# The end of a mixture-of-experts layer: residual rows read once and normed between the last expert products, and the last two experts' rows normed apart and stored by index

## The chip, the cores and the metric

The kernel runs on one core of one Trainium2 chip. The metric is the device time of one execution in microseconds (us): 1222.65 us, the median of three runs (1221.38 to 1224.46). The profile is of one further execution, which took 1224.64 us; the profiler's span of it is 1222.9 us. All rows below are from that execution, and their times count from the start of its span. Engines are named as the profile names them: PE is TensorE (PEld its weight loads), DVE is VectorE, ACT is ScalarE, POOL is GpSimd, SP is SyncE, which here only issues DMAs. A "q" behind a name is the engine's sequencer.

## The reference, cut to what matters

One layer over 1024 tokens of width 1024: a mixer, a cross-attention, then a mixture of 16 experts in 4 groups (each token goes to one group and to two experts in it), and a final RMSNorm. Only the last part matters here:

```
x   = x + sum over a token's two experts e of  weight * (silu(t @ w_gate[e]) * (t @ w_up[e])) @ w_down[e]
out = x / sqrt(mean(x * x) + 1e-6) * final_norm          # per token, over 1024 columns
```

Here t is the normed x. The two experts of a token lie in one group, so two experts of different groups never share a token.

## The kernel before, in words

**Experts.** Token rows of t lie in DRAM as `h3d`, the rows of x as `acd`; both are 1024 x 1024 float32 (plus spare rows). `ORDER` runs the experts as 0, 4, 8, 12, 1, 5, ... 11, 15, so neighbours are of different groups. Each expert has a first tile of up to 128 token rows and a second of up to 64 more; the second is computed inside `second(e)` (L1207), a branch that is taken only if the expert has more than 128 tokens. Row numbers are in `idi`, combine weights in `wts`; `slot(e, i)` (L1089) gives both columns for tile i. A row number past the end is left out by the DMA.

**One expert.** `fetch` gathers rows of `h3d` by an indirect DMA on POOL; `turned` transposes them on PE; `gate_up` (L1126) does 6 products of 512 columns for each of 8 weight tiles (48 in all), `hidden` the silu and the product, `over` (L1135) transposes the result into `hid`, `down` (L1143) does 6 products for each of 4 weight tiles (24). For the second tile the like are `gate_up2` (32 products), `hidden2`, `over2`, `down2` (16) and `rows2` (L1194). Every product is done as three, on operands split in a high and a low part (`split`, L173: the high part a copy on ACT, the low part a subtraction on DVE, 128 x 1024 each).

**Rows back.** `add_rows` (L1198) adds an expert's rows to `acd` by an indirect DMA on POOL that accumulates in DRAM. The framework orders whatever touches the same DRAM tensor, so an add waits until the one before it has landed. The loop over the first 15 experts is a software pipeline: while expert `ORDER[s]` is computed, the down products and adds of `ORDER[s-1]` are done (L1343 to L1359).

**Weights.** `Weights` (L1260) is a queue written out by hand: 9 raw tiles of 512 KB that SP loads in the order of `X.jobs`, and 28 slots for split pairs. `X.split(n)` splits the next n loaded tiles and so frees raw tiles for further loads; `X.get(key)` splits until the tile asked for is ready. The order of the jobs (L659 to L665) puts the last expert's gate and up tiles behind the down tiles of the one before. In this data the branches of expert 11 (called `p` at the end) are taken, those of 7 and 15 (`LAST`) are not.

**The end.** After the loop come p's down products and both adds (L1369 to L1381), then the last expert's gate, up and hidden (L1387 to L1395), then SP reads all of `acd` as eight row tiles `acc[t]` (L1402), then its down products. The last expert's rows are not added in DRAM: `placed` (L1433) puts them in place by products with a 0/1 matrix `oh`, 4 to 6 per half tile of 512 columns. Modes "A" and "B" alternate over the tiles: in "A" DVE adds the product to `acc` in SBUF and the norm works on `acc`; in "B" PE adds `acc` by one more product and the norm reads PSUM. `summed` (L1452) is a square with a row sum on ACT and two small operations on POOL (add EPS, power -0.5); `scaled` (L1464) multiplies by the root and by `final_norm` (`fn`) on DVE and SP stores the tile. All of this is under `manual_schedule`: each engine executes its own instructions in program order.

Of the kernel before, what the change touches and what calls it, by code (L numbers as in the profile page):

```python
# [8 lines left out]
F32 = mybir.dt.float32  # L9
F32R = mybir.dt.float32r  # L10
# [43 lines left out]
C_N = C_WR + ND * 24  # L54


MODES = "ABABABAB"
START = 12
FILL = 2
LAG = 2  # L60


class Slots:
# [22 lines left out]
def block_kernel(ctx: ExitStack, tc: tile.TileContext, A):  # L86
# [572 lines left out]
    for s, e in enumerate(ORDER):  # L659
        gu = [("gu", e, k) for k in range(ND)]  # L660
        dn = [("dn", ORDER[s - 1], k) for k in range(4)] if s else []
        for name, i, k in dn + gu if s == NE - 1 else gu + dn:
            W.add((name, i, k), A["w_" + name][i, k])
    for k in range(4):
        W.add(("dn", ORDER[-1], k), A["w_dn"][ORDER[-1], k])  # L665
# [541 lines left out]
    def second(e):  # L1207

        return tc.If((flags & (1 << e)) > 0, preferred_fallthrough_block=True)

    hrow = [half.get() for _ in range(2)]
    routed = half.get(BF16, (P, P))
    act.copy(routed, idf)
# [98 lines left out]
    with tc.manual_schedule():  # L1312
        flags = nc.values_load(two[0:1, 0:1], engines=(PE, ACT, DVE), min_val=0, max_val=(1 << NE) - 1)
        X = Weights(W.jobs, W.flying, W.ready, RAW)
        X.load()
        x0 = x0_bufs[0]
        run(turned(x0, xg[0]))
        with second(ORDER[0]):
            turned2()
        for i in range(2):  # L1320
            fetch(ORDER[1], i)
        pool.memset(og[1][LO], 0.0)
        for s, e in enumerate(ORDER[:-1]):
            p = ORDER[s - 1] if s else None
            nx = ORDER[s + 1]
            for k in range(ND):
                gate_up(x0, X.get(("gu", e, k)), k)
                X.split(1)
            hidden()
            ws = [X.get(("gu", e, k)) for k in range(ND)]  # L1330
            with second(e):
                for k in range(ND):
                    gate_up2(ws[k], k)
                hidden2(slot(e, 1)[1])
            for k in range(ND):
                X.drop(("gu", e, k))
            x0 = x0_bufs[(s + 1) % 2]
            ops = turned(x0, xg[0])
            if s + 2 < NE:
                fetch(ORDER[s + 2], 0)  # L1340
            run(ops)
            X.split(2)
            if p is not None:  # L1343
                wd = [X.get(("dn", p, k)) for k in range(4)]
                for k in range(4):
                    down(wd[k], k)
                X.split(1)
                weighted(slot(p, 0)[1])
                add_rows(slot(p, 0)[0], og[0])
            over()  # L1350
            X.split(2)
            if p is not None:
                with second(p):
                    for k in range(4):
                        down2(wd[k], k)
                    rows2(og[1])
                add_rows(slot(p, 1)[0][LO], og[1][LO])
                for k in range(4):
                    X.drop(("dn", p, k))  # L1359
            with second(e):  # L1360
                over2()
            with second(nx):  # L1362
                turned2()
            if s + 2 < NE:
                fetch(ORDER[s + 2], 1)


        p, LAST = ORDER[-2:]
        wd = [X.get(("dn", p, k)) for k in range(4)]  # L1369
        for k in range(4):  # L1370
            down(wd[k], k)
        X.split(1)
        weighted(slot(p, 0)[1])
        add_rows(slot(p, 0)[0], og[0])
        with second(p):
            for k in range(4):
                down2(wd[k], k)
            rows2(og[1])
        add_rows(slot(p, 1)[0][LO], og[1][LO])
        for k in range(4):  # L1380
            X.drop(("dn", p, k))  # L1381
        slots.put(*xg, *x0_bufs[NE % 2])
        fn, row = slots.get(), slots.get()
        oh = slots.get(F32R), slots.get(F32R)
        pool.iota(row, pattern=[[1, T]], base=0, channel_multiplier=0, allow_small_or_imprecise_dtypes=True)
        pool.dma_start(fn, A["final_norm"])
        for k in range(ND):  # L1387
            gate_up(x0, X.get(("gu", LAST, k)), k)
            X.split(2)
# [8 lines left out]
        assert not X.jobs  # L1398
        X.split(4)
        wd = [X.get(("dn", LAST, k)) for k in range(4)]  # L1400
        acc = [X.place(X.raw, F32) for _ in range(NT)]
        for t in range(NT):  # L1402
            sp.dma_start(acc[t], acd[cut(t), :])
        over()
        with second(LAST):
            over2()
        slots.put(*x0, xp)
        slots.free.extend(X.raw)
        ogs = [[slots.get(F32R) for _ in range(2)] for _ in range(2)]
        for i in range(2):  # L1410
            dve.tensor_scalar(oh[i], row, idf[:, LAST * 8 + i:LAST * 8 + i + 1], None, op0=ALU.is_equal)
        with second(LAST):
            for k in range(4):
                down2(wd[k], k)
            rows2(og[1])
            split(ogs[1][0][LO], ogs[1][1][LO], og[1][LO])
        for k in range(4):
            down(wd[k], k)
        for n in range(2):
            split(ogs[0][0][:, HS[n]], ogs[0][1][:, HS[n]], dn_banks[n], slot(LAST, 0)[1])  # L1420
        for k in range(4):
            X.drop(("dn", LAST, k))
        slots.free.extend(X.pair)
        slots.put(*og, hid, hp)
        banks.put(*gu_banks, *dn_banks, *turn_banks)

    ssf = const.tile([P, 2 * NT], F32, name="ssf")
    rf = const.tile([P, NT], F32, name="rf")  # L1430
    pss, jk = {}, {}

    def placed(t):  # L1433
        jk[t] = slots.get()
        pss[t] = [banks.get() for _ in range(2)]
        for n, ps in enumerate(pss[t]):
            pe.matmul(ps, oh[0][:, cut(t)], ogs[0][0][:, HS[n]], start=True, stop=False)
        with second(LAST):
            for n, ps in enumerate(pss[t]):
                for o in ogs[1]:  # L1440
                    pe.matmul(ps, oh[1][LO, cut(t)], o[LO, HS[n]], start=False, stop=False)
        for n, ps in enumerate(pss[t]):
            pe.matmul(ps, oh[0][:, cut(t)], ogs[0][1][:, HS[n]], start=False, stop=MODES[t] != "B")  # L1443
            if MODES[t] == "B":
                pe.matmul(ps, ident, acc[t][:, HS[n]], start=False, stop=True)  # L1445

    def added(t):
        if MODES[t] != "B":
            for n, ps in enumerate(pss[t]):
                dve.tensor_tensor(acc[t][:, HS[n]], ps, acc[t][:, HS[n]], op=ALU.add)  # L1450

    def summed(t):  # L1452
        r, s2 = rf[:, t:t + 1], [ssf[:, 2 * t + n:2 * t + n + 1] for n in range(2)]
        if MODES[t] == "B":
            for n, ps in enumerate(pss[t]):
                act.activation(jk[t][:, HS[n]], ps, AF.Square, scale=1.0 / 32.0, accum_out=s2[n])  # L1456
            pool.tensor_scalar(r, s2[0], s2[1], EPS, op0=ALU.add, op1=ALU.add)  # L1457
        else:
            act.activation(jk[t], acc[t], AF.Square, scale=1.0 / 32.0, accum_out=s2[0])
            pool.tensor_scalar(r, s2[0], EPS, None, op0=ALU.add)  # L1460
        pool.tensor_tensor(r, r, mhalf[:, 0:1], op=ALU.pow)
        slots.put(jk[t])

    def scaled(t):  # L1464
        r = rf[:, t:t + 1]
        if MODES[t] == "A":
            dve.scalar_tensor_tensor(acc[t], acc[t], r, fn, op0=ALU.mult, op1=ALU.mult)
        elif MODES[t] == "B":
            for n, ps in enumerate(pss[t]):
                dve.scalar_tensor_tensor(acc[t][:, HS[n]], ps, r, fn[:, HS[n]], op0=ALU.mult, op1=ALU.mult)  # L1470
        else:
            act.activation(acc[t], acc[t], AF.Copy, scale=r)
            pool.tensor_tensor(acc[t], acc[t], fn, op=ALU.mult)
        banks.put(*pss[t])
        sp.dma_start(A["out"][cut(t), :], acc[t])

    with tc.manual_schedule():
        for t in range(NT + LAG):
            if t < NT:
                placed(t)  # L1480
                added(t)
                summed(t)
            if t >= LAG:
                scaled(t - LAG)


def layout(inputs):
# [63 lines left out]
```

## Time and profile before

| | us |
|---|---|
| median of the runs | 1222.65 |
| the profiled execution | 1224.64 |
| its span | 1222.9 |
| PE busy in the span | 1178.0 (96%) |
| DVE busy | 712.3 (58%) |
| ACT busy | 567.5 (46%) |
| POOL busy | 188.6 (15%) |

How to read it: PE is busy nearly everywhere, but the share is a mean over all stages. The last 66 us, from the end of the loop over the experts on, are what the change touches; the table by stretches and the timelines below show them. A timeline row gives start, duration, engine, line, operation, what it writes and reads, how many instructions were merged, and in brackets the engine's idle time before it with what ended it.

### The profile page before, as it was taken

The page shows a single profiled execution, that of the slowest core. Times are in us where ns is not written, and L with a number is a line of the kernel's source. Part 1 is how long each engine was busy: PE and PEld are TensorE (multiplying, and loading weights), DVE is VectorE, ACT ScalarE, POOL GpSimd, SP SyncE. Part 2 cuts the span into 40 slices and gives each one's busy share as a digit, 9 for nine tenths or more (in the row PEclk, how much of TensorE's full clock was granted, in tenths as well). Part 3 has the DMA queues.
Part 4 walks back from the last instruction along what each step waited for, and adds up shares of the span by engine and source line. Part 5 has one row for each costly group of instructions (what it writes and reads, how often), then busy time and mean ns, then how long its engine had stood idle before and what let it go on. Part 6 is the DMA issues. An engine that isn't in the chain of part 4 may idle for free. (4 is left out here: it accounts for less than half of the span.)

```text
span 1222.9 us, 20592 instructions
## 1 busy us (share of the span) xinstructions
PE 1178.0 (96%) x7918; PEld 966.8 (79%) x7918; DVE 712.3 (58%) x1162; ACT 567.5 (46%) x965; POOL 188.6 (15%) x229
## 2 busy tenths in 40 slices
PE   9999999999999999999999999789999999999985
PEld 7787878787889988898888888568787777787762
DVE  6625454547457512364454776756867768668645
ACT  6613232323335402463244443545866767658633
POOL 1100101010100100100001333212223222123122
PEclk9999999999999999999999999889999999999988
DMA  9601110111426811120032321667979779798764
GB/s 343 240 18 48 41 54 35 36 53 54 157 85 242 281 63 35 35 104 1 1 121 83 125 104 70 218 232 242 317 245 377 254 263 349 255 338 290 247 176 194
DMA packets 58316, 196.48 MB, mean 161 GB/s; under 512 B 8925, under 2 KB 9565, under 8 KB 58208
## 3 DMA queue, kind: packets, MB, share of 16 engines
q1 hardware_dynamic: 45216, 157.69, 35.2%
q0 software_dynamic: 12704, 37.26, 10.4%
q8 instruction: 68, 1.11, 0.4%
q14 instruction: 40, 0.33, 0.1%
q10 hardware_dynamic: 288, 0.09, 0.0%
HBM read 173.49 MB, written 29.62 MB: 166 GB/s over the span
## 5 line engine op out<-in xcount | busy, mean ns | idle before, releaser
L257 PE MATMUL b<-s,s 128*128 128x512 f32 (+1 forms) x1056 | 402.7, 382 | 0.9 <-ACT s L165 0.8
L259 PE MATMUL b<-s,s 128*128 128x512 f32 (+1 forms) x1056 | 392.6, 372 | 0.0
L258 PE MATMUL b<-s,s 128*128 128x512 f32 (+1 forms) x1056 | 392.1, 371 | 0.1
L169 DVE TENSOR_TENSOR s<-s,s 128x1024 fp32r<-128x1024 f32 (+2 forms) x272 | 315.1, 1203 | 57.1 <-ACT s L163 35.4
L163 ACT CAST s<-s 128x1024 fp32r<-128x1024 f32 (+2 forms) x272 | 268.2, 1042 | 133.5 <-PE b L259 47.7
L1124 PE MATMUL b<-s,s 128*128 128x512 f32 x1152 | 275.3, 397 | 4.5 <-PEq L1362 1.7
L1124 PEld LDWEIGHTS b<-s,s 128*128 128x128 f32 x1152 | 217.0, 191 | 51.9 <-ACT s L163 2.7
L259 PEld LDWEIGHTS b<-s,s 128*128 128x128 f32 x1056 | 199.0, 188 | 35.4 <-issue 0.2
L257 PEld LDWEIGHTS b<-s,s 128*128 128x128 f32 x1056 | 199.0, 189 | 33.5 <-ACT s L165 1.5
L258 PEld LDWEIGHTS b<-s,s 128*128 128x128 f32 x1056 | 199.5, 189 | 31.3 <-DVE s L171 1.0
L169 DVE TENSOR_TENSOR s<-b,s 128x512 fp32r<-128x512 f32 (+1 forms) x112 | 70.9, 647 | 45.5 <-ACT s L163 42.5
L1200 POOL DMA_INDIRECT acd<-s,idi x30 | 59.2, 1972 | 204.9 <-ACT s L1148 66.4
L1163 PE MATMUL b<-s,s 128*128 128x512 f32 x384 | 90.5, 391 | 0.0
L1163 PEld LDWEIGHTS b<-s,s 128*128 128x128 f32 x384 | 71.6, 188 | 14.7
L163 ACT CAST s<-b 128x512 fp32r<-128x512 f32 (+1 forms) x112 | 60.7, 558 | 42.6 <-PE b L264 16.6
L1106 POOL DMA_INDIRECT s<-h3d,idi x32 | 37.1, 1160 | 106.4 <-PE b L1114 87.3
L1175 ACT COPY h<-b 64x512 f32<-64x512 f32 x32 | 18.6, 582 | 67.7 <-PE b L1163 57.0
L1176 DVE TENSOR_TENSOR h<-b,h 64x512 f32<-64x512 f32 x16 | 10.9, 682 | 63.1 <-ACT h L1175 63.1
L784 DVE TENSOR_TENSOR s<-b,s 128x512 f32<-128x512 f32 x16 | 11.0, 691 | 58.7 <-PE b L259 58.6
L264 PE MATMUL b<-ident,s 128*128 128x128 f32 x288 | 40.9, 273 | 1.0 <-DVE s L615 0.9
L547 DVE TENSOR_TENSOR s<-s,s 128x512 f32<-128x512 f32 x28 | 19.3, 691 | 37.6 <-PE b L538 22.1
L264 PEld LDWEIGHTS b<-ident,s 128*128 128x128 f32 x288 | 34.5, 140 | 8.0 <-DVE s L615 1.3
(232 smaller groups left out, 920.2 us busy)
## 6 DMA issues: line engine op xcount, KB each, us to landing
s<-in_w_gu_dram SPq DMA_DIRECT2D x128, 512.0 KB, 6.8
s<-in_w_dn_dram SPq DMA_DIRECT2D x64, 512.0 KB, 7.5
s<-in_w_in_dram SPq DMA_DIRECT2D x26, 512.0 KB, 3.5
s<-in_w_kv_dram SPq DMA_DIRECT2D x16, 512.0 KB, 5.5
h3d<-s POOLq DMA_DIRECT2D x9, 512.0 KB, 3.1
acd<-s POOLq DMA_DIRECT2D x9, 512.0 KB, 3.2
s<-in_xT_dram SPq DMA_DIRECT2D x16, 256.0 KB, 5.5
s<-in_x_dram SPq DMA_DIRECT2D x8, 512.0 KB, 9.0
```

The source lines that it names most:

```text
L163: act.copy(hi, src)
L169: (eng or dve).tensor_tensor(lo, src, hi.bitcast(F32), op=ALU.subtract)
L257: pe.matmul(ps, lh, rh, start=first, stop=False)
L258: pe.matmul(ps, lh, rl, start=False, stop=False)
L259: pe.matmul(ps, ll, rh, start=False, stop=last)
L264: pe.transpose(pt[:, cut(c)], src[:, cut(half * 4 + c)], ident)
L547: dve.tensor_tensor(k4[:, :, 0, :], k4[:, :, 0, :], tv[:, :, 1:2].to_broadcast([P, nb, w]), op=ALU.mult)
L1106: pool.indirect_dma_start(out=to, out_offset=None, in_=h3d, in_offset=rows, bounds_check=T - 1, oob_is_err=False)
L1124: pe.matmul(ps[n], l, r[:, HS[n]], start=a, stop=b)
L1163: pe.matmul(ps[n], l, r[:, HS[n]], start=first and i == 0, stop=last and i == 1)
L1175: act.copy(up2[UP], ps[UP])
L1200: pool.indirect_dma_start(out=acd, in_=src, in_offset=None, compute_op=ALU.add, out_offset=rows, bounds_check=T - 1, oob_is_err=False)
```

## The change

The order of the jobs in the weight queue becomes gate and up before down for the last expert too. In the last round of the loop the two splits behind `over` go. After the loop the last expert's gate and up products come first, with one split for each weight tile instead of two; when nothing is left to load and five raw tiles are free, SP is given the eight reads of `acd` (into four slots that the loop no longer needs and four raw tiles), and POOL the load of `final_norm`. Then the end goes as follows. POOL gathers three row tiles out of `acd`: p's first tile and the last expert's first tile (`ax[0]`, `ax[1]`), and one tile `ax2` whose lower half are p's second rows and whose upper half the last expert's second rows (`ix2`). The products with `oh` are gone, as are p's two adds into `acd`. In the code below `residual` has SP read `acd` into `acc`; `root` is POOL's two operations (a sum with EPS and a power); `final` calls `summed` for each tile of its list and `scaled` one tile behind; `first_out` scales one `ax[j]` on DVE and calls `store`; `second_out` scales the two halves of `ax2` on DVE, each in its expert's branch, and calls `store` once. A row that neither p nor LAST touches is final in `acc`; all eight tiles of `acc` are normed and stored, and the rows of p and LAST are then stored once more, over them, by three indirect DMAs on POOL. All tiles are normed in mode "A".

```diff
-MODES = "ABABABAB"
+MODES = "AAAAAAAA"
...
-        for name, i, k in dn + gu if s == NE - 1 else gu + dn:
+        for name, i, k in gu + dn:
...
-            X.split(2)
+            if nx != ORDER[-1]:
+                X.split(2)
...
+        def squares(a, ss):
+            act.activation(jk[0:a.shape[0], 0:a.shape[1]], a, AF.Square, scale=1.0 / 32.0, accum_out=ss)
+
+        def summed(t):
+            squares(acc[t], ssf[:, t:t + 1])
+            root(rf[:, t:t + 1], ssf[:, t:t + 1])
+
+        def scaled(t):
+            r = rf[:, t:t + 1]
+            if MODES[t] == "A":
+                dve.scalar_tensor_tensor(acc[t], acc[t], r, fn, op0=ALU.mult, op1=ALU.mult)
...
+            sp.dma_start(A["out"][cut(t), :], acc[t])
...
+        def first_sum(j, e):
+            a, ss, r = ax[j], [ssf[:, NT + 2 * j + n:NT + 2 * j + n + 1] for n in range(2)], rf[:, NT + j:NT + j + 1]
+            for n in range(2):
+                dve.scalar_tensor_tensor(a[:, HS[n]], dn_banks[n], slot(e, 0)[1], a[:, HS[n]],
+                                         op0=ALU.mult, op1=ALU.add)
+                squares(a[:, HS[n]], ss[n])
+            root(r, *ss)
+
+        def second_sum(j, e, wd):
+            part = UP if j else LO
+            with second(e):
+                for k in range(4):
+                    down2(wd[k], k)
+                for n in range(2):
+                    act.copy(up2[UP], gu1_banks[n][UP])
+                    dve.tensor_tensor(og[1][part, HS[n]], gu1_banks[n][LO], up2[UP], op=ALU.add)
+                dve.tensor_tensor(ax2[part], ax2[part], og[1][part], op=ALU.add)
+                act.activation(jk[part], ax2[part], AF.Square, scale=1.0 / 32.0, accum_out=c1[0][0][part])
+
+        def store(ix, src):
+            rows = bass.IndirectOffsetOnAxis(ap=ix, axis=0)
+            pool.indirect_dma_start(out=A["out"], in_=src, in_offset=None, out_offset=rows,
+                                    bounds_check=T - 1, oob_is_err=False)
...
+            X.split(1)
+            if not X.jobs and len(X.raw) >= 5 and len(acc) == 4:
+                residual(range(4))
+                acc += [X.place(X.raw, F32) for _ in range(4)]
+                residual(range(4, NT))
+                fn = X.place(X.raw, F32)
+                pool.dma_start(fn, A["final_norm"])
...
         X.split(4)
...
+        for ix, to in (slot(p, 0)[0], ax[0]), (slot(LAST, 0)[0], ax[1]), (ix2, ax2):
+            pool.indirect_dma_start(out=to, out_offset=None, in_=acd,
+                                    in_offset=bass.IndirectOffsetOnAxis(ap=ix, axis=0))
+        for k in range(4):
+            down(wd[k], k)
         over()
+        first_sum(0, p)
+        second_sum(0, p, wd)
         with second(LAST):
             over2()
...
+        final(range(0, 4))
+        second_sum(1, LAST, wl)
+        root(c1[1], c1[0][0])
         for k in range(4):
...
+            down(wl[k], k)
+        final(range(4, NT))
+        first_out(0, p)
+        second_out()
+        first_sum(1, LAST)
+        first_out(1, LAST)
```

## Rows read from the trace of the kernel before

**Rows 1.** The table by stretches for three stretches of the last 53 us: length, then busy time (and instructions) of PE, PEld, DVE, ACT and POOL, then PE's granted clock, the DMA share and GB/s.
```profile
1170.00:1180.00 10.00, 8.17 (x34) 5.81 (x32) 8.31 (x9) 8.58 (x10) 3.56 (x3) 1.00 0.36 55
1180.00:1190.00 10.00, 6.41 (x19) 4.91 (x20) 4.92 (x6) 0.88 (x2) 1.75 (x3) 0.66 0.83 222
...
1210.00:1223.00 13.00, 0.99 (x3) 0.16 (x1) 4.19 (x6) 1.57 (x6) 2.47 (x4) 0.74 0.39 161
```
**Rows 2.** The timeline of PE: a gate and up of 48 products, the transposes of `over`, those of `over2`, p's 24 down products and its 16 of the second tile, and the 24 down products of the last expert.
```profile
1107.55 11.16 PE L1124 MATMUL b<-s,s 128*128 128x512 f32 x48 [0.27 <-PEq L1362]
...
1155.26 0.60 PE L1139 MATMUL b<-ident,h 128*128 128x128 f32 x4
1156.27 0.46 PE L1188 MATMUL b<-ident,h 64*128 64x64 f32 x4 [0.41 <-PEq L1353]
1157.14 5.95 PE L1124 MATMUL b<-s,s 128*128 128x512 f32 x24 [0.42 <-ACT s L163]
1162.93 3.79 PE L1163 MATMUL b<-s,s 128*128 128x512 f32 x16
...
1184.71 7.73 PE L1124 MATMUL b<-s,s 128*128 128x512 f32 x24 [0.72 <-ACTq L1405]
```
**Rows 3.** The timeline of the norm of the first tile, of mode "A": the square on ACT and POOL's two operations.
```profile
1196.05 1.06 ACT L1459 ACTIVATE s<-s 128x1024 f32<-128x1024 f32 x1 [2.53 <-DVE s L1450]
...
1197.30 0.24 POOL L1460 TENSOR_SCALAR rf<-ssf 128x1 f32<-128x1 f32 x1 [15.54 <-ACT s L1459]
...
1197.62 0.58 POOL L1461 TENSOR_TENSOR rf<-rf,mhalf 128x1 f32<-128x1 f32 x1
```
**Rows 4.** The timeline of DVE and POOL at the end of the norms: L1467 scales a tile of mode "A" (both inputs in SBUF), L1470 two halves of mode "B" (one input in PSUM).
```profile
1210.18 1.40 DVE L1470 SCALAR_TENSOR_TENSOR s<-b,rf,s 128x512 f32<-128x512 f32 x2
...
1210.40 0.22 POOL L1460 TENSOR_SCALAR rf<-ssf 128x1 f32<-128x1 f32 x1 [1.97 <-ACT s L1459]
...
1211.50 1.28 DVE L1467 SCALAR_TENSOR_TENSOR s<-s,rf,s 128x1024 f32<-128x1024 f32 x1
...
1211.82 1.13 POOL L1457 TENSOR_SCALAR rf<-ssf 128x1 f32<-128x1 f32 x1 [0.55 <-ACT s L1456]
1213.03 0.56 POOL L1461 TENSOR_TENSOR rf<-rf,mhalf 128x1 f32<-128x1 f32 x1
1213.62 1.41 DVE L1470 SCALAR_TENSOR_TENSOR s<-b,rf,s 128x512 f32<-128x512 f32 x2 [0.84 <-POOL rf L1461]
```
**Rows 5.** Instructions of the kernel's closing line (L1547) by engine: count, shortest, median and longest in ns, first and last start; then what SP waited for in the last part: in all, times, longest.
```profile
L1547 POOLq DRAIN  x3: 46/109/9029, 1213.0 to 1222.6; - x3
...
SPq L1547 <- PEq L1547: 4.6, 2, 4.1
...
SPq L1547 <- DMA out_dram<-s: 1.9, 1, 1.9
```
**Rows 6.** The timeline of POOL around the last adds into `acd`.
```profile
1156.89 2.15 POOL L1200 DMA_INDIRECT acd<-s,idi  x1 [15.51 <-ACT s L1148]
1167.85 1.43 POOL L1200 DMA_INDIRECT acd<-s,idi  x1 [8.81 <-DMA acd<-s,idi]
1171.11 1.56 POOL L1200 DMA_INDIRECT acd<-s,idi  x1 [1.82 <-DMA acd<-s,idi]
...
1180.58 1.17 POOL L1386 DMA_DIRECT2D s<-in_final_norm_dram  x1
```
**Rows 7.** From the views by line, the times from issue to landing (shortest, median, longest, in us) with the line's issues: the add at 1167.85 alone, one gather of `h3d` while little else is moved, two gathers back to back under load, the eight reads of `acd`, and the stores of `out`.
```profile
L1200 POOL DMA_INDIRECT acd<-s,idi x1: 1434/1434/1434, 1167.9 to 1167.9; - x1
...
DMA to landing us min/median/max: 2.5/2.5/2.5
...
L1106 POOL DMA_INDIRECT s<-h3d,idi x1: 1039/1039/1039, 1100.8 to 1100.8; - x1
...
DMA to landing us min/median/max: 4.3/4.3/4.3
...
L1106 POOL DMA_INDIRECT s<-h3d,idi x2: 982/1012/1043, 1071.4 to 1072.7; - x2
...
DMA to landing us min/median/max: 6.3/7.0/7.8
...
L1403 SPq DMA_DIRECT2D s<-acd x8: 326/540/872, 1183.5 to 1188.0; - x8
...
DMA to landing us min/median/max: 5.6/8.2/10.1
...
L1475 SPq DMA_DIRECT2D out_dram<-s x8: 332/332/451, 1201.6 to 1215.1; - x8
...
DMA to landing us min/median/max: 2.6/2.7/3.3
```
**Rows 8.** Groups of instructions by line from 1105 to 1182 us (busy time, mean ns of one, idle before): the splits of weights, and the copy and the sum of a second tile.
```profile
L169 DVE TENSOR_TENSOR s<-s,s 128x1024 fp32r<-128x1024 f32 x38 | 44.0, 1216 | 1.4 <-ACT s L163 0.8 <-DVEq L1362 0.6
...
L1175 ACT COPY h<-b 64x512 f32<-64x512 f32 x6 | 3.5, 582 | 10.7 <-PE b L1163 7.2 <-DVE s L1176 3.5
L1176 DVE TENSOR_TENSOR s<-b,h 64x512 f32<-64x512 f32 x4 | 2.7, 683 | 9.3 <-DMA acd<-s,idi 7.9 <-ACTq L1360 0.7 <-ACT h L1175 0.7
```
**Rows 9.** From the view by line, as in rows 7, the earlier plain stores of 512 KB into `acd` from POOL.
```profile
L1029 POOL DMA_DIRECT2D acd<-s x8: 589/589/602, 665.5 to 766.4; - x8
...
DMA to landing us min/median/max: 2.9/3.2/5.5
```

More of the change, by code (lines that the diff above doesn't have):

```diff
@@ L1209, in second @@
         return tc.If((flags & (1 << e)) > 0, preferred_fallthrough_block=True)
+    ssf = const.tile([P, NT + 8], F32, name="ssf")
+    rf = const.tile([P, NT + 4], F32, name="rf")
+    ix2 = const.tile([P, 1], I32, name="ix2")
+    pool.memset(ssf, 1.0)
     hrow = [half.get() for _ in range(2)]
@@ L1368, in block_kernel @@
         p, LAST = ORDER[-2:]
[L1369 to L1381, printed above, removed]
-        slots.put(*xg, *x0_bufs[NE % 2])
@@ L1383, in block_kernel, with residual @@
[L1383 to L1386, printed above, removed]
+        assert p // 4 != LAST // 4
+        slots.put(*xg, *x0_bufs[NE % 2])
+        acc = [slots.get() for _ in range(4)]
+        dve.tensor_copy(ix2[LO], slot(p, 1)[0][LO])
+        dve.tensor_copy(ix2[UP], slot(LAST, 1)[0][LO])
+        def residual(ts):
+            for t in ts:
+                sp.dma_start(acc[t], acd[cut(t), :])
@@ new lines, in root @@
+        def root(r, *ss):
+            if len(ss) == 2:
+                pool.tensor_scalar(r, ss[0], ss[1], EPS, op0=ALU.add, op1=ALU.add)
+            else:
+                pool.tensor_scalar(r, ss[0], EPS, None, op0=ALU.add)
+            pool.tensor_tensor(r, r, mhalf[0:r.shape[0], 0:1], op=ALU.pow)
+        def squares(a, ss):
[3 more added lines that the diff above has]
+            root(rf[:, t:t + 1], ssf[:, t:t + 1])
@@ new lines, in scaled, with final @@
+        def scaled(t):
+            r = rf[:, t:t + 1]
+            if MODES[t] == "A":
+                dve.scalar_tensor_tensor(acc[t], acc[t], r, fn, op0=ALU.mult, op1=ALU.mult)
+            else:
+                act.activation(acc[t], acc[t], AF.Copy, scale=r)
+                pool.tensor_tensor(acc[t], acc[t], fn, op=ALU.mult)
+            sp.dma_start(A["out"][cut(t), :], acc[t])
+        def final(ts):
+            for i, t in enumerate(ts):
+                summed(t)
+                if i:
+                    scaled(ts[i - 1])
+            scaled(ts[-1])
@@ new lines, in block_kernel @@
+        c1 = [ssf[:, NT + 4 + n:NT + 5 + n] for n in range(2)], rf[:, NT + 2:NT + 3]
+        def first_sum(j, e):
[5 more added lines that the diff above has]
+            root(r, *ss)
@@ new lines, in store, with first_out, second_out @@
+        def store(ix, src):
+            rows = bass.IndirectOffsetOnAxis(ap=ix, axis=0)
+            pool.indirect_dma_start(out=A["out"], in_=src, in_offset=None, out_offset=rows,
+                                    bounds_check=T - 1, oob_is_err=False)
+        def first_out(j, e):
+            dve.scalar_tensor_tensor(ax[j], ax[j], rf[:, NT + j:NT + j + 1], fn, op0=ALU.mult, op1=ALU.mult)
+            store(slot(e, 0)[0], ax[j])
+        def second_out():
+            for part, e in ((LO, p), (UP, LAST)):
+                with second(e):
+                    dve.scalar_tensor_tensor(ax2[part], ax2[part], c1[1][part], fn[part], op0=ALU.mult, op1=ALU.mult)
+            store(ix2, ax2)
@@ L1387, in block_kernel @@
         for k in range(ND):
             gate_up(x0, X.get(("gu", LAST, k)), k)
-            X.split(2)
+            X.split(1)
[5 more added lines that the diff above has]
+                pool.dma_start(fn, A["final_norm"])
+        assert not X.jobs and len(acc) == NT
         hidden()
@@ L1397, in block_kernel @@
             X.drop(("gu", LAST, k))
-        assert not X.jobs
         X.split(4)
[L1400 to L1403, printed above, removed]
+        wd, wl = ([X.get(("dn", e, k)) for k in range(4)] for e in (p, LAST))
+        slots.free.extend((*X.pair, *X.raw))
+        jk = slots.get()
+        ax, ax2 = [slots.get() for _ in range(2)], slots.get()
+        for ix, to in (slot(p, 0)[0], ax[0]), (slot(LAST, 0)[0], ax[1]), (ix2, ax2):
+            pool.indirect_dma_start(out=to, out_offset=None, in_=acd,
+                                    in_offset=bass.IndirectOffsetOnAxis(ap=ix, axis=0))
@@ L1404, in block_kernel @@
+        for k in range(4):
+            down(wd[k], k)
         over()
+        first_sum(0, p)
+        second_sum(0, p, wd)
         with second(LAST):
             over2()
[L1407 to L1416, printed above, removed]
@@ L1417, in block_kernel @@
-        for k in range(4):
[L1418 to L1484, printed above, removed]
+        final(range(0, 4))
+        second_sum(1, LAST, wl)
+        root(c1[1], c1[0][0])
+        for k in range(4):
+            down(wl[k], k)
[4 more added lines that the diff above has]
+        first_out(1, LAST)
```

1 line of the change is left out of this document (removed).

## The prediction

> **What bounds the kernel now.** I read the table by stretches first. PE is busy until about 1180 us; from 1180 to 1190 it works 6.4 of 10 us at a granted clock of 0.66, and in the last 13 us it does almost nothing [rows 1]. The change touches only this end, so I went on to the timeline there. After the loop PE starts p's down products at 1157.1; the last expert's down products end near 1192.4, after 7.7 us where 24 products took 5.95 before [rows 2]. Then come the products that put rows in place, with the norms beside them: the first tile's square starts at 1196.05 [rows 3], DVE's last scaling ends at 1213.62 + 1.41 = 1215.0 [rows 4]. The span, though, is 1222.9. The closing line says why: POOL's drain begins at 1213.0 and takes 9.03 us, and SP, done with its stores, waits 4.1 us for the others [rows 5]. So the end hangs on POOL: its last operation ends at 1213.03 + 0.56 = 1213.6 [rows 4], and the span ends 9.3 us behind that. I write E = 9.3 us for this.
>
> **The change, step by step**, on the clock of this execution.
>
> *1. PE's order.* Gate and up of the last expert start where p's down products started, 1157.1. By count of the queue 5 of its 8 tiles are split by then and 11 splits are left; at 1.2 us each on DVE [rows 8] the sixth is ready near 1161, and PE needs it at 1157.1 + 5 x 1.4 = 1164. So the fewer splits cost nothing; their cover is the 11.2 us of gate and up. Without it PE would wait 1.2 us a tile. Then: 48 products 11.2 [rows 2] to 1168.3; a branch not taken 0.4, as PE's gap at a branch [rows 2]; p's 24 products 5.7 (5.95 with a wait in it) to 1174.4; `over` 0.6; branch 0.4; p's second tile 3.8 to 1179.2 [rows 2]. The stall and the half clock of rows 1 go, as do the placing products and p's two adds.
>
> *2. The reads of `acd`.* They are issued early but wait for the last add, expert 7's second. That add starts at 1167.85, lands 2.5 us later [rows 7], and POOL's next work starts at 1171.1 [rows 6]: 0.7 us from landing to start, which I use for every such wait. Before, the reads went at 1183.5 [rows 7], so they gain 12 us. On POOL the three gathers stand behind this add and the load of `final_norm` (1.2 us, done in the wait); they take 1.0 each with 0.3 between. A gather lands after 4.3 us on quiet queues and after 6.3 and 7.8 back to back under load [rows 7]; here 4 MB of reads and the load of `final_norm` go beside it, so I take 7.5 for the first: 1178.6, the third near 1182.5. The ends, 4.3 and 10.1 (the longest read of `acd` under its own load [rows 7]), shift what follows by -3 and +3.
>
> *3. p's sums.* DVE's two halves 2 x 0.7 (the form with one input in PSUM [rows 4]) to 1180.1, the square of the second half 0.8 to 1180.9. Queued behind it on ACT: a branch 0.4, two copies of 0.6 alternating with DVE's two sums of 0.7 [rows 8] to 1183.9, the addition to `ax2` 1.2 (nearest row: a split [rows 8]), its square 1.25, two branches 0.8. So ACT reaches the first tile's square at **1187.0**; before it was 1196.05. The last expert's down products wait for DVE's reading until 1180.1 and end by 1188 even at the slow 7.7 us: off the path.
>
> *4. Eight norms.* Square 1.06, POOL's two operations and their gaps 1.1 [rows 3]: scaling starts at 1189.2. Now all tiles are of mode "A". DVE's scaling of that mode (1.28, both inputs in SBUF) began at 1211.50; POOL's small operation of the next tile began 0.3 later and took 1.13, to 1212.95, just past DVE's end; beside the "B" form the same operation took 0.22 [rows 4]. So in a row of "A" tiles POOL's first operation waits out each scaling, and DVE then waits for POOL's power: 1.27 + 0.17 + 0.58 + gaps of 0.1 = 2.1 a tile, where ACT could feed one in 1.06. The root of `ax2`, queued on POOL after the fourth, adds 0.9. The last scaling ends at 1189.2 + 7 x 2.1 + 0.9 + 1.3 = **1206.1**, 8.9 ahead of before. Mildly read, one row could be chance: then 1.27 a tile, and 6.7 less in the sum. The Trainium skill ("SBUF — State Buffer", "SBUF: two separate sides" and "Who interferes with whom") has the pair of ports that VectorE and GpSimd share as an exclusive lock for the whole instruction, taken by a VectorE instruction with two SBUF inputs against a GpSimd one that reads SBUF, and held by whichever is first. By that rule POOL could also win, DVE would wait 0.3 first, and a tile would take 2.3: 1.4 more in the sum.
>
> *5. The stores by index.* They write `out`, which SP's eight stores write too, so the first waits for the last of these: 2.7 and 0.7 [rows 7, 6] to 1209.5. No row shows a plain store by index. Bounds: 2.5 us to land (an add of nearly no rows) and 4.3 (a gather on quiet queues) [rows 7]; a plain store of 512 KB from POOL lands in 3.2 with 0.6 of issue [rows 9]. With a gather's issue of 1.0 I take 3.6, nearest to that store. First: 1209.5 to 1213.1, and 0.7. Second, made to wait as the adds are [rows 6]: issued 1213.8 to 1214.8. Only now does POOL get to the last expert's root, 0.9 with gaps 1.1, to 1215.9, as it stands behind both stores; DVE's scaling 1.3 to 1217.2; the third store 0.3 + 1.0, to **1218.5** (the second lands near 1217). Everything else of this part (p's scalings, the last expert's sums) fits into the wait for the first landing.
>
> *6. The end.* 1218.5 + E 9.3 = 1227.8, against 1222.9: +4.9. The execution's own time lies 1.7 above its span and 2.0 above the median; I put the difference on the median: **1227.6**. The norms end 8.9 earlier, but POOL's last operation, which was 1.4 ahead of DVE's last scaling, is now 12.4 behind it.
>
> **The rivals.**
>
> *A. POOL isn't held* behind the scaling. Then step 4 takes 1.27 a tile and the end is 6.7 earlier, 1220.9: not slower. It decides if POOL's first operation beside a scaling takes 0.2 instead of 1.1. For it: one row only. Against it: the operation ended with DVE's.
>
> *B. The three stores don't wait for each other*, only for SP's. Then 1209.5, two issues with a gap 2.3, root 1.0, scaling 1.3, third issue 1.3: 1215.4, or 3.1 less, 1224.5. Against it: adds into `acd` of disjoint rows do wait, 8.8 and 1.8 us [rows 6]. The Trainium skill ("DMA: Bandwidth & Descriptors", "Two DMAs through the same engine are not ordered") says that only the completion semaphore orders two DMAs, one queue being no substitute; the rows of the adds agree.
>
> *C. The drain doesn't trail POOL's last operation.* If it is over when the third store has landed (1217.5 + 3.6), with 0.4 for SP and 0.8 for the closing barrier, the span is 1222.3: 1222.1. For it: no row tells what the drain does. Against it: no DMA of POOL was under way then, and it still took 9.
>
> *D. The gathers starve* behind the reads of `acd` and come last of all, 1171.1 + 10.1 + four blocks of 1.3 = 1186.4, 3.9 later: 1231.5.
>
> *E. Two of A to C together*, as A and B: 1217.8.
>
> **How the numbers follow.** A difference of 0.3%, 3.7 us, is about what a measurement of this kernel can tell from none: faster is under 1219.0, slower over 1226.3. Forecast 0.46, A 0.12, B 0.12, C 0.13, D 0.07, E 0.10. The forecast's own range is 1223.5 to 1231.5 (the gathers' 3 both ways, 0.7 for each landing); 0.35 of its 0.46 is slower, the rest the same. A: 0.08 same, 0.04 faster. B: 0.08 same, 0.03 slower, 0.01 faster. C: 0.11 same, 0.02 faster. D slower, E faster. Sums: faster 0.17, same 0.38, slower 0.45. From 1219.0 to 1232.0 lie the forecast, most of A, B and C, and half of D.
>
> **What would show it.** Right: the first square near 1187; POOL's small operations over 1 us and scalings about 2.1 apart; POOL waiting on landings of `out`; the last scaling 12 us ahead of POOL's last store; a drain of some 9 us behind that. Wrong: scalings 1.3 apart (A), stores issued back to back (B), a short drain (C), sums waiting for a gather past 1182 (D). A first square far from 1187 would make steps 2 and 3 wrong.

## The result and the profile after

The changed kernel takes 1233.4 us (median of 4 runs, 1232.8 to 1234.9), the kernel before on the same chip 1223.2 (1221.4 to 1224.5): a ratio of 1.0082, 95% interval 1.0069 to 1.0095. It is slower, by 10.1 us where 4.9 were forecast, and lies above the range. All medians here and below are of fast runs; one execution of run r2, which took 5789 us, is not among them. The profiled execution has a span of 1233.1 us against 1222.9.

**Where to lay the two traces side by side.** The last piece of PE's work ahead of the edited code is the transposes of `over2` [rows 2]; there the changed kernel is already late. I call the time from their first product to the end of the span the *tail*: 1222.9 - 1156.27 = 66.6 us before, 1233.1 - 1158.24 = 74.9 after, 8.2 more. The other 1158.24 - 1156.27 = 2.0 us arise ahead of the edit (r4 and a5 look at them). PE's timeline after, as in [rows 2]:

```profile
1158.24 0.46 PE L1187 MATMUL b<-ident,h 64*128 64x64 f32 x4 [0.41 <-PEq L1357]
1159.06 11.16 PE L1123 MATMUL b<-s,s 128*128 128x512 f32 x48 [0.36 <-ACTq L1357]
1170.37 5.70 PE L1123 MATMUL b<-s,s 128*128 128x512 f32 x24
...
1176.26 3.88 PE L1162 MATMUL b<-s,s 128*128 128x512 f32 x16
1184.76 8.28 PE L1123 MATMUL b<-s,s 128*128 128x512 f32 x24 [4.61 <-DVE s L1419]
```

Gate and up, p's down products and its second tile follow one another as step 1 has them. The last expert's 24 wait 4.6 us until DVE has read the bank; that wait and the lower granted clock they meet (0.66 on average from 1180 to 1190) lie off the path, as norms run meanwhile. The table by stretches, as in [rows 1]:

```profile
1170.00:1180.00 10.00, 9.85 (x45) 7.83 (x44) 5.49 (x6) 4.14 (x5) 5.55 (x5) 1.00 0.60 192
1180.00:1190.00 10.00, 5.39 (x13) 4.00 (x13) 3.69 (x5) 2.60 (x6) 0.88 (x2) 0.66 1.02 407
1210.00:1223.00 13.00, 0.00 (x0) 0.00 (x0) 5.42 (x6) 1.44 (x4) 3.52 (x5) 0.50 0.27 107
1223.00:1233.00 10.00, 0.00 (x0) 0.00 (x0) 0.00 (x0) 0.00 (x0) 0.48 (x1) 0.50 0.13 51
```

From 1180 to 1190 the DMA engines are full (share 1.02, 407 GB/s) and every compute engine is under 60% busy: data is late. The last 10 us hold 0.5 us of POOL and no other compute engine. What is late from 1180 to 1190, in POOL's timeline (the add of expert 7's second tile, `final_norm`, the three gathers; [rows 6] before):

```profile
1169.13 2.79 POOL L1199 DMA_INDIRECT acd<-s,idi  x1 [8.12 <-DMA s<-in_w_dn_dram]
1171.41 1.16 POOL L1458 DMA_DIRECT2D s<-in_final_norm_dram  x1
1175.16 1.10 POOL L1474 DMA_INDIRECT s<-acd,idi  x1 [2.59 <-DMA acd<-s,idi]
1176.57 0.94 POOL L1474 DMA_INDIRECT s<-acd,idi  x1 [0.30 <-PE b L1138]
1177.81 0.94 POOL L1474 DMA_INDIRECT s<-acd,ix  x1 [0.30 <-issue]
```

and their landings, from the views by line of the add alone, then of the gathers:

```profile
DMA to landing us min/median/max: 5.2/5.2/5.2
```
```profile
DMA to landing us min/median/max: 8.7/9.9/11.2
```

The add before took 1.43 to issue and 2.5 to land [rows 6, 7]; here it is 2.79 and 5.2. Its bracket names a load of weights, but the add ahead of it landed only at 1158.85 + 9.5 = 1168.35, 0.8 us before it starts. The norms, in the timeline of DVE and POOL ([rows 4] before):

```profile
1193.80 1.28 DVE L1401 SCALAR_TENSOR_TENSOR s<-s,rf,s 128x1024 f32<-128x1024 f32 x1 [3.50 <-POOL rf L1389]
...
1194.07 1.09 POOL L1388 TENSOR_SCALAR rf<-ssf 128x1 f32<-128x1 f32 x1 [0.31 <-ACT s L1392]
...
1195.84 1.28 DVE L1401 SCALAR_TENSOR_TENSOR s<-s,rf,s 128x1024 f32<-128x1024 f32 x1 [0.76 <-POOL rf L1389]
1195.89 1.31 POOL L1388 TENSOR_SCALAR rf<-ssf 128x1 f32<-128x1 f32 x1
...
1209.06 1.28 DVE L1401 SCALAR_TENSOR_TENSOR s<-s,rf,s 128x1024 f32<-128x1024 f32 x1 [0.76 <-POOL rf L1389]
```

Scalings stand 2.04 apart, and POOL's 128x1 operation ends 0.08 us behind the scaling it began in. Then the stores by index, the landing of the third, and POOL's drain on the closing line ([rows 5] before):

```profile
1214.12 1.09 POOL L1437 DMA_INDIRECT out_dram<-s,idi  x1 [5.09 <-DVE s L1419]
1218.49 0.98 POOL L1437 DMA_INDIRECT out_dram<-s,ix  x1 [3.28 <-DMA out_dram<-s,idi]
...
1222.42 1.06 POOL L1437 DMA_INDIRECT out_dram<-s,idi  x1 [1.91 <-DVE s L1441]
```
```profile
DMA to landing us min/median/max: 3.4/3.4/3.4
```
```profile
L1555 POOLq DRAIN  x3: 46/109/10037, 1222.2 to 1232.8; - x3
```

DVE's last of eight scalings ended at 1210.3; the issue of POOL's last store ends at 1223.48, and the span 9.6 us behind that. The store had landed by 1222.42 + 3.4 = 1225.8, 7.3 us ahead of the end.

### The profile page after: what moved, and what is told of

It reads as the page before. It is cut to its first block, busy times and chain, and to the rows that moved or that the text cites. A ratio compares the mean times of both kernels' runs of the same rounds, so it can differ in the third digit from the quotient of the medians.

```text
span 1233.1 us, 20486 instructions
## 1 busy us (share of the span) xinstructions
PE 1162.1 (94%) x7870; PEld 959.7 (78%) x7870; DVE 712.0 (58%) x1156; ACT 568.8 (46%) x963; POOL 199.0 (16%) x239
## 5 line engine op out<-in xcount | busy, mean ns | idle before, releaser
L1199 POOL DMA_INDIRECT acd<-s,idi x28 | 54.9, 1960 | 198.3 <-ACT s L1147 78.3
```

The lines of the kernel that those rows point to most:

```text
L1199: pool.indirect_dma_start(out=acd, in_=src, in_offset=None, compute_op=ALU.add, out_offset=rows, bounds_check=T - 1, oob_is_err=False)
```

## The experiments

Eleven kernels and a repeat of the changed one, in four groups on one chip each. Ratios are to the kernel before on the same chip; the tail is from each profile, so of one execution.

| run | median us | ratio (95%) | tail us |
|---|---|---|---|
| before | 1223.2 to 1224.4 | 1 | 66.6 |
| changed | 1233.4 | 1.0082 (1.0069, 1.0095) | 74.9 |
| a5_again: changed | 1233.9 | 1.0081 (1.0068, 1.0095) | 74.6 |
| r1: final_norm in PSUM | 1227.5 | 1.0026 (1.0015, 1.0037) | 69.8 |
| r2: reads behind gathers | 1227.0 | 1.0023 (1.0013, 1.0034) | 68.7 |
| r3: one store of three | 1227.6 | 1.0027 (1.0016, 1.0039) | 70.8 |
| r4: idle products | 1231.1 | 1.0059 (1.0047, 1.0071) | 73.1 |
| c1: r1 and r2 | 1222.3 | 0.9993 (0.9984, 1.0002) | 64.3 |
| d1: final_norm later | 1233.8 | 1.0076 (1.0062, 1.0090) | 74.5 |
| d2: c1, final_norm later | 1222.4 | 0.9994 (0.9984, 1.0003) | 65.0 |
| e1: a split later | 1230.4 | 1.0057 (1.0043, 1.0071) | 72.4 |
| e2: c1 and e1 | 1221.5 | 0.9982 (0.9973, 0.9991) | 62.9 |
| b1: before, a POOL write last | 1227.1 | 1.0032 (1.0019, 1.0044) | 70.4 |
| b2: before, two roots off POOL | 1219.4 | 0.9968 (0.9956, 0.9979) | 62.0 |

How far a tail can be trusted: the same code gave 74.9 and 74.6 (changed, a5). Before and b1 have the same code up to DVE's last scaling, which ends 58.8 and 58.0 us after `over2`. So less than 1 us between two tails shows nothing by itself. The medians of r1 to r4 lie 0.4 to 1.0 us under the expected ranges: these were reckoned from the changed kernel's 1233.4, and the profiles of r1 to r4 reach `over2` 2.1 to 4.0 us before its own.

**r1: is POOL held by DVE's scalings?**

```
+        for n in range(2):
+            act.copy(gu_banks[n], fn[:, HS[n]])
...
-                dve.scalar_tensor_tensor(acc[t], acc[t], r, fn, ...)
+                    dve.scalar_tensor_tensor(acc[t][:, HS[n]], gu_banks[n], r, acc[t][:, HS[n]], ...)
```

(and the same in `first_out` and `second_out`)

> The changed kernel with final_norm copied into two PSUM banks, so that DVE's scaling of a tile reads one operand from SBUF and one from PSUM, in two halves (0.70 us each for such a pair in rows 4). Theory (POOL's root is held by a DVE instruction with two SBUF inputs): the scalings follow each other at about 1.45 us instead of 2.05, POOL's 128x1 add takes under 0.4 us instead of 1.31, the last of eight scalings ends some 4.5 us earlier and the kernel takes 1228.5 to 1229.5 us instead of 1233.4. Rival (the tiles are paced by ACT's squares or by the chain itself): the pace stays near 2 us and the time within 1 us of 1233.4.

Timeline of DVE (four tiles as eight halves), then of POOL:

```profile
1192.00 5.36 DVE L1402 SCALAR_TENSOR_TENSOR s<-b,rf,s 128x512 f32<-128x512 f32 x8 [3.50 <-POOL rf L1389]
```
```profile
1192.28 0.22 POOL L1388 TENSOR_SCALAR rf<-ssf 128x1 f32<-128x1 f32 x1 [0.31 <-ACT s L1392]
1192.58 0.57 POOL L1389 TENSOR_TENSOR rf<-rf,mhalf 128x1 f32<-128x1 f32 x1
```

POOL's operation, begun 0.28 us into a scaling, takes 0.22 instead of 1.09 to 1.31, and a tile 5.36 / 4 = 1.34 instead of 2.04. The tail falls by 5.1. The hold is shown, with its price. Rival A had POOL not held: r1 runs that way, the changed kernel does not.

**r2: what makes the gathers late?**

```
-                residual(range(4))
-                residual(range(4, NT))
...
+        residual(range(NT))        # behind the gathers, and on pool instead of sp
```

> The changed kernel with the eight reads of acd issued by POOL right behind the three gathers, instead of by SP ahead of them. Theory (the gathers land late because 4 MB of reads are in flight beside them): they land 4.3 to 5 us after issue, near 1179.5, 1181 and 1182.5 in place of 1183.8, 1186.4 and 1189.0; the reads take POOL some 1.0 us each, so that its first root comes near 1187.5 in place of 1192.7, and the kernel takes 1228 to 1229 us. Rival (the gathers are slow by themselves behind the add, 8 to 11 us): they land as before, the reads come later still, and the kernel is slower than 1233.4.

The view by line of the gathers:

```profile
DMA to landing us min/median/max: 5.1/6.0/6.8
```

The first lands at 1177.4, the third at 1182.4. POOL's first root of a tile, in the changed kernel and in r2:

```profile
1192.90 0.22 POOL L1388 TENSOR_SCALAR rf<-ssf 128x1 f32<-128x1 f32 x1 [5.71 <-ACT s L1392]
```
```profile
1186.32 0.22 POOL L1388 TENSOR_SCALAR rf<-ssf 128x1 f32<-128x1 f32 x1 [1.75 <-ACT s L1392]
```

Of these 6.6 us 2.1 lie ahead of `over2`; 4.5 are left. The gathers land after 5.1 to 6.8 us instead of 8.7 to 11.2, so it was the 4 MB beside them that made them late. The add ahead of them landed after 4.3 us here and not 5.2, so they also start 0.7 sooner against `over2`. The tail falls by 6.2: these 4.5 (0.7 of them the add's) and 1.7 of a shorter drain, which no theory had (last section).

**r3: what do the stores cost in turn, and does the end follow POOL?**

```
-        first_out(0, p)
-        second_out()
+        first_out(0, p, False)      # normed, not stored
+        second_out(False)
```

(the output lacks these rows; the run is for its time alone)

> The changed kernel without two of its three stores by index: expert 11's rows and the joined second tiles are normed but not stored, only LAST's first tile is. Theory (each store waits for the landing of the one before, and the program ends 9.6 us after POOL's last instruction): the one store is issued near 1217 instead of 1222.4, and the time falls by 5 to 5.5 us, to 1228 to 1228.5, with the distance from POOL's last instruction to the end still 9.3 to 9.7. Rival (the stores overlap, or the end is set by something else): the time falls by under 2 us, or the distance changes.

```profile
1214.46 1.09 POOL L1437 DMA_INDIRECT out_dram<-s,idi  x1 [1.61 <-DVE s L1441]
```
```profile
L1557 POOLq DRAIN  x3: 46/109/9917, 1214.2 to 1224.7; - x3
```

POOL's last operation ends 1225.0 - 1215.55 = 9.45 us ahead of the end, within the expected 9.3 to 9.7. Set against `over2`, the store comes 3.9 us earlier and the tail is 4.1 shorter. That is less than the 5 to 5.5 expected: without the two stores POOL waits 6.34 us at its last root for ACT's squares, which stand behind DVE's scalings and the last expert's sums. The spans of the two profiles differ by 8.1; the other 4.0 lie ahead of `over2`.

**r4 and a5: the 2 us ahead of the edit.**

```
+        busy(gu_banks[0], 10)       # r4: between turned and turned2
...
+        busy(gu_banks[0], 8)        # r4: behind turned2
```

> The changed kernel with 18 idle bf16 products of 128x256 put on PE between the transposes of the first expert's rows and its first gate/up product, where PE waits 1.05 us and less. Theory (1.6 of the 10 us come from TensorE's clock, which in the changed kernel's profile is granted at half speed from 783.9 to 787.1 and in the profile of before is not): the first 48 gate/up products take 11.2 us instead of 12.8, and the kernel 1231.5 to 1232. Rival (that stretch differs by run and not by kernel, or the products themselves delay the start): 1233 to 1234.

> The changed kernel once more, unchanged, beside the others on one chip. Theory (the 1.9 us that its first profile was late at the first gate/up products of the expert loop belong to that one execution): the new profile shows those 48 products in 11.2 us instead of 12.8 and the span comes out near 1231; the ratio to the kernel before stays at 1.007 to 1.009. Rival (they belong to the changed kernel): 12.8 us again, and a ratio near 1.008 of which the start keeps its 1.9 us.

PE's timeline at the first gate and up of the expert loop, of before, of changed, of a5:

```profile
783.37 11.18 PE L1124 MATMUL b<-s,s 128*128 128x512 f32 x48
```
```profile
783.61 12.77 PE L1123 MATMUL b<-s,s 128*128 128x512 f32 x48
```
```profile
783.71 12.77 PE L1123 MATMUL b<-s,s 128*128 128x512 f32 x48
```

and the table from 783 to 788, of before and of changed:

```profile
783.00:788.00 5.00, 5.00 (x28) 4.16 (x26) 3.81 (x5) 4.52 (x6) 1.91 (x2) 1.00 0.97 315
```
```profile
783.00:788.00 5.00, 5.00 (x20) 4.03 (x21) 3.83 (x5) 4.29 (x5) 2.12 (x3) 0.66 0.94 338
```

In the changed kernel the granted clock is at 1.2 GHz from about 783.9 to 787.3 (0.66 over these 5 us), after PE had stood waiting 1.05 us for DVE's split just before; the kernels in which it stays at 2.4 GHz wait there too (before 1.06, r1 1.05). At the end of these products the changed kernel is 1.83 of its 1.97 us late. My theory, that this belongs to one execution, fell: a5 shows it again. But r1 to r3, with the same code up to there and no filling, show 11.2 as r4 does, so r4 does not test the filling. The granted clocks of all runs say a little more: of the 14 runs of changed, a5 and d1, eight have a mean clock of 0.974 or 0.975 and take 1234.2 us on average, six have 0.976 or 0.977 and take 1232.3. So it looks like something that comes in a bit over half of the executions and costs 1.9 us; that it is this stretch is shown in three profiles only. It need not belong to these kernels: beside r1, the kernel before has seven executions at a clock of 0.986 with 1225.4 us on average and nine at 0.989 or 0.990 with 1223.2. And the profiles without it reach `over2` at 1154.2 (r3) to 1157.3 (b1), so 2 us between two single profiles tell little there. What brings it on stays open.

**c1: do the two costs add?** r1 and r2 together.

> The changed kernel with both earlier edits: final_norm in PSUM for the scalings, and the eight reads of acd issued by POOL behind the gathers. Theory (the two costs lie one after the other: the gathers' lateness sets the start of the norms, the hold of POOL their pace): the gains of the two, 5 and 6 us after taking off how early each profile was at the end of the expert loop, add to 10 to 11, and the kernel takes 1221.5 to 1223.5 us, at or just below the kernel before. Rival (the reads, landing one each 1.3 us until 1192.5, set the pace once the hold is gone): no better than 1225.

They nearly do: the tail is 10.5 shorter than in the changed kernel, against 5.1 + 6.2 = 11.3 for the two alone, and 2.3 shorter than before; the median is level with before (the interval holds 1).

**d1, d2: why does the add land late?** `final_norm` is read behind the gathers instead of ahead of them.

> The changed kernel with the read of final_norm moved on POOL's queue from ahead of the three gathers to behind them, so that nothing of POOL's is in flight beside expert 7's second add. Theory (the 512 KB of final_norm, issued 2.3 us behind the add, hold up its landing: 4.7 to 5.2 us where the kernel before has 2.5): the add lands 2.5 to 3 us after its start, reads and gathers start some 2 us earlier, the first tile's square too, and the kernel takes 1231 to 1232 us instead of 1233.4 to 1233.9. Rival (the last weights, still landing until the add is issued, hold it up, or it is slow by its own size): it lands after 4.5 us or more again, and the time stays.

> The changed kernel with final_norm in PSUM and the reads of acd on POOL behind the gathers, as in the run that had both, and final_norm read between the gathers and those reads. Theory (final_norm holds up the add): 1.5 to 2 us off that run's 1222.3, so 1220.3 to 1221. Rival (the add is held up by something else): 1222 to 1223, as final_norm now comes 1.3 us ahead of every read of acd.

The theory fell in both: the add, with nothing of POOL's beside it, takes 2.64 and 3.34 to issue and lands after 4.4 and 5.2. What still stood beside it was DVE's row of splits, so:

**e1, e2: is the add's issue held by DVE's splits?**

```
             gate_up(x0, X.get(("gu", LAST, k)), k)
-            X.split(1)
+            if k < ND - 1:
+                X.split(1)
```

> The changed kernel without the last of the eight splits that stand beside the last expert's gate and up products: it joins the four behind them. In the changed kernel's profile DVE runs eight splits without a gap until 1170.6, two SBUF inputs each, and POOL's issue of expert 7's second add, begun at 1169.1, ends 1.3 us behind them. Theory (the issue is held by DVE's splits as the roots are by the scalings): with the splits over 1.2 us earlier against the products, the issue takes 1.4 to 1.8 us instead of 2.8, the add lands some 1.2 us earlier, and the first tile's square with it; 1 to 1.5 us in the time. Rival (the add's issue and landing are slow by themselves, or by the weights in flight): over 2.4 us of issue and the same landing.

> The changed kernel with final_norm in PSUM, the reads of acd on POOL behind the gathers, and the last split moved as in the run beside this one. Theory: some 1.2 us below the 1222.3 and 1222.4 of the two runs with the first two edits, so about 1221.1, with POOL's last store 1.2 us earlier against the last expert's products. Rival: 1222.3 again.

DVE's timeline in the changed kernel and in e1, POOL's in e1, and the add's landing in e1:

```profile
1161.43 9.18 DVE L168 TENSOR_TENSOR s<-s,s 128x1024 fp32r<-128x1024 f32 x8
```
```profile
1159.38 8.04 DVE L168 TENSOR_TENSOR s<-s,s 128x1024 fp32r<-128x1024 f32 x7
```
```profile
1167.19 1.54 POOL L1199 DMA_INDIRECT acd<-s,idi  x1 [8.23 <-DMA s<-in_w_dn_dram]
1168.23 1.15 POOL L1459 DMA_DIRECT2D s<-in_final_norm_dram  x1
```
```profile
DMA to landing us min/median/max: 2.6/2.6/2.6
```

In the changed kernel the issue starts at 1169.13, DVE's splits end at 1170.61, and the issue ends 1.3 behind them. In e1 they end 0.2 us into it: 1.54 us of issue, and a landing after 2.6, with `final_norm` in flight as before. The tail falls by 2.5, and in e2 by 1.4 against c1. More speaks for the hold: of the eleven profiles with the new order ten have the issue end 1.30 to 1.32 us behind the last split of the row, though it starts between 0.1 and 2.0 us ahead of that end. The eleventh is r4, with all eight splits (DVE, POOL, the landing):

```profile
1159.15 9.17 DVE L168 TENSOR_TENSOR s<-s,s 128x1024 fp32r<-128x1024 f32 x8
```
```profile
1166.72 1.78 POOL L1199 DMA_INDIRECT acd<-s,idi  x1 [7.99 <-DMA s<-in_w_dn_dram]
```
```profile
DMA to landing us min/median/max: 3.0/3.0/3.0
```

Against `over2` the issue starts 0.13 us earlier than in the changed kernel and the splits end at the same time, but the issue ends only 0.2 behind them. The add lands after 3.0, and the tail is 1.7 shorter, though nothing of r4's edit stands there. So POOL need not wait for the whole row, and the price of the hold depends on how the issue falls beside it: against e1 it is 1.3 in the issue and 2.6 in the landing of the changed kernel, 0.2 and 0.4 in r4's. Why the landing loses more than the issue isn't shown.

**b1, b2: what sets the end of the kernel before?**

```
+        pool.memset(acc[NT - 1][:, 0:1], 0.0)     # b1: behind the last store to out
...
-        pool.tensor_tensor(r, r, mhalf[:, 0:1], op=ALU.pow)
+        if t < NT - 2:                             # b2, and its add likewise
+            pool.tensor_tensor(r, r, mhalf[:, 0:1], op=ALU.pow)
...
+            dve.tensor_scalar(r, s2[0], s2[1], EPS, op0=ALU.add, op1=ALU.add)
...
+        act.activation(rf[:, t:t + 1], rf[:, t:t + 1], AF.Sqrt)
...
+            dve.reciprocal(r, r)
```

> The kernel before with one 128x1 memset on POOL behind everything: it overwrites a column of the last tile after the tile's store to out has read it, so it waits for that landing, some 3.3 us after DVE's last scaling, and does no other work. Theory (the end follows POOL's last instruction by 9.3 us, whatever the other engines do): POOL's last instruction moves from 1213.6 to about 1218.8 and the kernel takes 5 us longer, 1228 to 1229. Rival (the end is set by the last store to out, and POOL's 9 us only happen to end with it): under 1 us longer.

> The kernel before with the roots of its last two tiles taken off POOL: DVE adds the epsilon, ACT takes the square root (its table loaded in ACT's idle time before), DVE the reciprocal; the order of DVE's scalings is kept, and they should end within 0.5 us of where they did. Theory (the end follows POOL's last instruction): that instruction is now the root of the sixth tile, some 4 us earlier, and the kernel ends when the stores to out have landed, 2 to 3.5 us earlier than before, at 1219.5 to 1221.5. Rival (something else holds the end): within 1 us of before, or slower by what the small DVE instructions add.

POOL's timeline in b1 and its last operation in b2; DVE's last scaling in b2; the closing lines of b1 and b2; what SP waited for in b2:

```profile
1218.36 0.10 POOL L1485 MEMSET s<- 128x1 f32 x1 [4.50 <-issue]
```
```profile
1206.71 0.56 POOL L1464 TENSOR_TENSOR rf<-rf,mhalf 128x1 f32<-128x1 f32 x1
```
```profile
1212.37 1.41 DVE L1485 SCALAR_TENSOR_TENSOR s<-b,rf,s 128x512 f32<-128x512 f32 x2
```
```profile
L1548 POOLq DRAIN  x3: 46/109/8537, 1218.3 to 1227.5; - x3
```
```profile
L1567 POOLq DRAIN  x3: 46/109/9029, 1206.7 to 1217.4; - x3
```
```profile
SPq L1567 <- DMA out_dram<-s: 1.9, 2, 1.6
SPq L1567 <- PEq L1567: 0.7, 2, 0.5
```

Against `over2`, b1's 0.1 us of work moves POOL's last operation by 3.85 us and the end by 3.8: the end follows POOL. It is not the expected 5, as DVE's last scaling ends 0.75 earlier there than in before and the write ends 3.2 behind it, where 3.8 were expected. In b2 POOL's last operation comes 5.8 us earlier and the end 4.7, of which 0.7 is DVE's, whose last scaling ends that much earlier against `over2`. The drain is over by 1206.7 + 9.0 = 1215.7, 2.0 ahead of the end, and DVE's last scaling ends 3.9 ahead of it. SP now waits for a landing of `out`, 1.6 at longest, and 0.5 for the other engines where it was 4.1 before [rows 5]: the last store to `out` is the end. b2 beats both kernels, and e2 is 0.18% faster than before.

## Why the prediction was wrong

**The step that failed is 2**, "The reads of `acd`", in two of its sizes. The first is the add. "That add ... lands 2.5 us later" was a row of an add with DVE idle beside it [rows 6, 7]; in the new order DVE splits weights there, and it took 5.2. Taken on the clock of before (less 2.0), it landed at 1172.4 instead of 1170.4. The trace of before has both cases, with DVE idle up to 1170.59 and with an add beside splits:

```profile
1170.59 0.68 DVE L1176 TENSOR_TENSOR s<-b,h 64x512 f32<-64x512 f32 x1 [7.88 <-DMA acd<-s,idi]
...
1173.05 9.17 DVE L169 TENSOR_TENSOR s<-s,s 128x1024 fp32r<-128x1024 f32 x8 [0.39 <-ACT s L163]
```
```profile
1178.00 2.12 POOL L1200 DMA_INDIRECT acd<-s,idi  x1 [5.33 <-DVE s L169]
```

Beside splits an issue took 2.12, as against 1.43. I had the lock of DVE and POOL in step 4, for POOL's arithmetic, and did not ask what else POOL issues beside a DVE instruction of two SBUF inputs. The second size is the gathers beside the reads. Of the first I wrote "I take 7.5"; it was 8.7, and 11.2 for the third, above the end of 10.1. The third landed at 1187.0 on the clock of before where I had 1182.5 (the step does not work this out; issues 1.3 apart and 7.5 to land give 1181.2): 2.0 of the lateness is the add's, 2.5 the gathers' own, which r2 puts down to the reads.

The Trainium skill ("SBUF — State Buffer", "Who interferes with whom") infers that such a `tensor_tensor` does not hold up the making of descriptors. Here the whole issue of an indirect DMA was held up by one (2.79 us, against 1.54 in e1); whether the making of descriptors waits, or the reading of the row numbers from SBUF, no run separates.

**The rest of the sum**, in the profiled execution. The first tile's square in ACT's timeline:

```profile
1191.65 1.06 ACT L1392 ACTIVATE s<-s 128x1024 f32<-128x1024 f32 x1 [0.17 <-ACTq L1481]
```

It came at 1191.65 - 2.0 = 1189.7, 2.7 behind 1187.0. From there the eight norms were 0.4 shorter than forecast, the stores 0.7 longer, E 0.3 longer: 2.7 - 0.4 + 0.7 + 0.3 = 3.3, and 4.9 + 3.3 = 8.2, the tail's growth. Where the add lands after 2.6, in e1, the tail grows by 5.7 against the forecast 4.9.

**A term that was not in the sum** is the 2.0 us ahead of the edit, which I took to be equal. They make the span's 10.2 of the tail's 8.2.

**By steps.** 1 was right (second tile's end 1180.1 - 2.0 = 1178.2, forecast 1179.2). 3 was right in size: 7.8 us from the first gather to the first square, forecast 8.4. 4 was right, 2.05 us a tile with 0.95 for the root of `ax2`. DVE always went first, as the rows had it: of the Trainium skill's rule that step 4 cites ("SBUF — State Buffer", "Who interferes with whom") this shows the one case, and the other, POOL first, did not occur beside a scaling. 5 was right in kind: each store lands after 3.1 to 3.5 us (3.6 taken) and the second waits for the first. Its sum has a slip: by its own numbers the third store could not start before 1213.8 + 3.6 + 0.7 = 1218.1, and it has 1217.5. These 0.6 are about the 0.7 that the stores took longer. In the run the second had landed 0.2 ahead of DVE's scaling, and the third waited for DVE. 6 was right: 9.6 for 9.3, and b1 moves the end with one write.

**The rivals.** A is refuted by POOL's 1.09 to 1.31 beside the scalings, and r1 gives its price; B by the second store's wait of 3.28 us for the first landing (and r3); C by b1 and by the third store, landed 7.3 us ahead of the end; and with them E. D, given 0.07, is nearest: the third gather landed at 1187.0 on that clock, D had 1186.4. Its reason was half right, as 2.0 of the lateness is the add's. That its 8.8 us come close to the tail's 8.2 is partly luck: its 3.9 count from 1182.5, though in step 3 the addition to `ax2` stood at 1183.9 anyway, so a landing at 1186.4 would cost 2.5.

## What to carry to other kernels

A landing time read from one place holds only for what runs beside it there: in a new order, look at which DVE instructions will overlap every POOL issue, and at what else is in flight. Ask which instruction of POOL is the last: here one write of 0.1 us, placed 3.85 us later, costs 3.8, and taking two roots off POOL makes the kernel before 0.32% faster. Compare traces from the last unedited instruction on, so that what the clock did before it is not booked on the edit.

## What the runs showed of the hardware beyond that

POOL's drain has a few lengths that repeat to within 7 ns: 9.03 us in before and b2, 10.03 or 10.04 in the changed kernel, a5, r1, r4, d1 and e1, 8.32 or 8.33 in r2, c1, d2 and e2, where POOL itself issues the eight reads of `acd`. Two lengths come once: b1, with one write more than before, has 8.54, and r3, with two stores less than the changed kernel, 9.92. The four kernels r2, c1, d2 and e2 end 7.9 us behind POOL's last operation instead of 9.6. What sets the length was not tried.
